# Gate and up projections of a SwiGLU FFN as 2x2 block products by Strassen's scheme, with the residual kept in DRAM meanwhile

## Chip, cores, metric

One Trainium2 chip, one of its cores. The metric is the time of one execution on the device, in microseconds. The median of three runs of the kernel before is 1309.06 us.

## The reference

One inference step of one layer on 512 prompt tokens and 8 sample tokens (520 columns together): dilated window attention and an RWKV-7 recurrence on the same normalised input, merged by gates, an output projection, and then the FFN that the change is about:

```python
x = x + mix
hn = rms_norm(x, lw['norm_ffn'])
ffn = (jax.nn.silu(hn @ lw['w_gate']) * (hn @ lw['w_up'])) @ lw['w_down']
return x + ffn
```

All is float32. `w_gate` and `w_up` are 1024 x 2816, `w_down` is 2816 x 1024; the last step is another RMS norm.

## The kernel before

Activations lie with features on the 128 partitions and the NT = 520 tokens on the free axis; a product is made in two chunks of CH = 260 columns (`CS[0]`, `CS[1]`). KD = 8 is the number of 128-row blocks of 1024, KF = 22 that of 2816.

Every float32 factor is split into a high part rounded to `fp32r` and a low part, and a product is the sum of three passes: high by high, high by low, low by high (`gemm_chunk`). One output tile of 128 features over 1024 inputs is thus 2 chunks x 8 blocks x 3 passes = 48 matmuls, each with its own weight load of 128 x 128 and 260 moving columns.

The work of TensorE is a list of `Job`s that `play` goes through: while it multiplies job i, it fetches the raw weights of job i+2 (`wraw`: one DMA of 512 KB on SP's queue, two buffers) and splits those of job i+1 (`wsplit`: ScalarE copies raw to `whi`, VectorE subtracts to `wlo`; two pairs of buffers). Behind a job comes its `post`, which takes the result from PSUM. Side chains (norms, for one) are generators that `Weave` mixes into the list by planned times; `wv.set` and `wv.until` are its flags. Instructions of one engine run in the order written down for it at build time, and semaphores between engines do the rest.

The end of the kernel in order:

- `w_out`, 8 jobs. `wo_pre` loads the input into `x2` (8 DMAs on POOL's queue), `wo_post` adds the product to `x2`, writes a scaled split of it into the last 8 blocks of the FFN's buffers `fh`/`fl` (`ff["h"]`, `ff["l"]`), and adds up the squares.
- `norm2`, a side chain: the reciprocal root `rs`, then for each of 8 blocks `x2 * g * rs` (VectorE, tile `hf`) and its split into `h2h`/`h2l`, the low part in turn on VectorE and on GpSimd (POOL).
- gate and up, 22 tiles each, alternately. The first EARLY = 3 pairs don't wait for `norm2`: they multiply the split from `wo_post`, and `rs` is multiplied in afterwards. The other 19 pairs multiply `h2h`/`h2l`. `gt_post` makes silu from tanh (ScalarE) and one VectorE operation for each chunk; `up_post` multiplies by the up result and splits the product into `fh`/`fl`.
- `w_down`, 8 output tiles over 22 blocks; `down_post` adds to `x2`, and `final` normalises and stores.

All operations go through one helper, so that the profile gives line 380 for every one of them; the tiles' names tell them apart. In the profile `sl` is the silu tile, `mm`, `ax` and `ch` are PSUM banks.

Of the kernel before, what the change touches and what calls it, by code (L numbers as in the profile page):

```python
# [8 lines left out]
FP = mybir.dt.float32  # L9
# [30 lines left out]
MERGE_AT = -1  # L40
SAMPLE_AT = -1
PLAIN = 4
EARLY = 3
FETCH = 2
SOLVERS = 2
RAWS = 4
# [419 lines left out]
def program(tc, I, O):  # L466
# [29 lines left out]
    def bank():  # L496
        return axp.tile([128, 512], FP, name=nm("ax"), tag="ax", bufs=3)
# [48 lines left out]
            E.matmul(ps[:cols, :n], lhsT=hi[:, k, :cols], rhs=b, start=False, stop=False)  # L546
            E.matmul(ps[:cols, :n], lhsT=lo[:, k, :cols], rhs=a, start=False, stop=(last and k == nk - 1))

    def play(jobs, more=None):
        raws, ws = {0: first_raw, 1: second_raw}, {0: first_w}  # L550

        def fetch(i, j):
            while len(jobs) <= max(i, j) and more:
# [1161 lines left out]
                                   op0=ALU.mult, op1=ALU.subtract)  # L1715
        return post

    mctx, fctx = ExitStack(), ExitStack()
# [27 lines left out]
    def wo_post(n):  # L1746
        def post(ps):
            x2 = ff["x2"]
            for c in range(2):
                V.tensor_tensor(out=x2[:, n, CS[c]], in0=x2[:, n, CS[c]], in1=ps[c][:, :CH], op=ALU.add)  # L1750

            g = feat[:, F_FFN, n:n + 1]
            S.activation(out=ff["h"][:, K0 + n], in_=x2[:, n], func=AF.Copy, scale=g)
            V.scalar_tensor_tensor(out=ff["l"][:, K0 + n], in0=x2[:, n], scalar=g, in1=ff["h"][:, K0 + n].bitcast(FP),
                                   op0=ALU.mult, op1=ALU.subtract)
            sumsq(ff["acc"], x2[:, n], n)
            if n == KD - 1:
                wv.spawn(norm2())
        return post

    def norm2():
        mctx.close()
        hp2 = ff["hp2"] = pool("h2", h2ctx, side="right")
        hh2 = ff["hh"] = hp2.tile([128, KD, NT], FR, name="h2h")
        hl2 = ff["hl"] = hp2.tile([128, KD, NT], FR, name="h2l")
        banks = yield from norm_r(ff["xp"], [ff["acc"]], slice(0, NT), TB, "f")
        for a, b, pb in banks:
            S.copy(out=ff["rs"][:, a:b], in_=pb[:, :b - a])
        wv.set("rs2")
# [13 lines left out]

    def gt_post(n):
        def post(ps):
            xp = ff["xp"]
            t = ff["t", n] = xp.tile([128, NT], FP, name=nm("sl"), tag="sl", bufs=2)
            for c in range(2):
                g = ps[c][:, :CH]
                if n < EARLY:  # L1790
                    gs = xp.tile([128, CH], FP, name=nm("g0"), tag="g0")
                    V.tensor_tensor(out=gs[:], in0=g, in1=ff["rs"][:, CS[c]], op=ALU.mult)
                    g = gs[:]
                S.activation(out=t[:, CS[c]], in_=g, func=AF.Tanh, scale=0.5)
                V.scalar_tensor_tensor(out=t[:, CS[c]], in0=t[:, CS[c]], scalar=1.0, in1=g, op0=ALU.add, op1=ALU.mult)
        return post

    def up_post(n):
        def post(ps):
            t = ff["t", n]  # L1800
            for c in range(2):
                V.tensor_tensor(out=t[:, CS[c]], in0=t[:, CS[c]], in1=ps[c][:, :CH], op=ALU.mult)
            if n < EARLY:
                V.tensor_tensor(out=t[:], in0=t[:], in1=ff["rs"][:], op=ALU.mult)
            S.activation(out=ff["h"][:, n], in_=t[:], func=AF.Copy, scale=0.5)
            V.scalar_tensor_tensor(out=ff["l"][:, n], in0=t[:], scalar=0.5, in1=ff["h"][:, n].bitcast(FP),
                                   op0=ALU.mult, op1=ALU.subtract)
# [160 lines left out]
```

## Time and profile before

| what | value |
|---|---|
| median of 3 runs | 1309.06 us (1307.44 to 1310.26) |
| the profiled execution | 1316.53 us, of which the span from first to last instruction is 1314.8 us |
| granted TensorE clock, mean of the span | 0.983 |
| matmuls in the span | 11738 |
| matmuls that read `h2h` or `h2l` | 1824 (3 x 608), first start 954.4 us, last start 1171.9 us |

PE is TensorE's matmuls, PEld its weight loads, DVE VectorE, ACT ScalarE, POOL GpSimd, SP the engine whose queue loads the weights. In rows of the timeline the first number is the start in us, the second the duration in us, and what stands in brackets is the idle time before and what ended it. In rows of groups, the number behind x is the count, then come busy us and mean ns, and behind the last bar the engine's idle time before them. Records of VectorE overlap by some 0.08 us where one operation follows another without a wait, so its throughput is read from the distance between starts.

### The profile page before, as it was taken

What the parts mean: (1) busy time and instruction counts of PE and PEld (TensorE: products, weight loads), DVE (VectorE), ACT (ScalarE), POOL (GpSimd) and SP (SyncE); (2) the same over time, 40 slices, a digit from 0 to 9 for tenths busy, and PEclk for the clock granted to TensorE, in tenths of its full rate; (3) what the DMA queues carried; (4) which work ended last, traced back from release to release, by engine and by line L of the source; (5) the groups of instructions that cost most, each with busy time, mean ns of one, the idle gap of its engine ahead of it and who ended that gap; (6) DMA issues with size and microseconds to landing.
All of it is one profiled execution on the core that took longest, in us unless ns stands there. A gap on an engine that the chain in (4) does not pass through costs nothing.

```text
span 1314.8 us, 29468 instructions
## 1 busy us (share of the span) xinstructions
PE 1264.7 (96%) x11738; PEld 1197.5 (91%) x11738; DVE 843.7 (64%) x2221; ACT 610.6 (46%) x1554; POOL 175.0 (13%) x261
## 2 busy tenths in 40 slices
PE   7999999999989989999999999999999999999996
PEld 7998999989978878888888888999999999999996
DVE  6956866954869998886986665555843444332333
ACT  5244244366656656675785665334433232222220
POOL 1300100100223332121123122110200000000000
PEclk9999999999989999997999999999999999999998
DMA  6523654634245554543245454552222222223331
GB/s 215 158 94 96 213 178 146 221 112 172 69 131 136 152 147 141 143 156 97 77 139 168 123 175 157 182 192 85 81 97 97 97 89 89 97 93 89 89 101 65
DMA packets 92137, 169.48 MB, mean 129 GB/s; under 512 B 42416, under 2 KB 47568, under 8 KB 92000
## 3 DMA queue, kind: packets, MB, share of 16 engines
q1 hardware_dynamic: 60880, 102.46, 24.6%
q0 software_dynamic: 14512, 46.47, 11.5%
q10 hardware_dynamic: 16608, 18.68, 4.3%
q8 instruction: 92, 1.51, 0.5%
q14 instruction: 45, 0.37, 0.1%
HBM read 133.20 MB, written 27.94 MB: 123 GB/s over the span
## 4 chain that ended last, share of the span: by engine, by line
PE 64%; DVE 15%; issue 9%; DMA 6%; ACT 4%; POOL 1%; SPq 1%; ACTq 0%; DVEq 0%; POOLq 0%
PE mm L380 51%; PE ax L380 8%; PE ch L380 5%; DVE wlo L380 2%; DVE X L380 1%; DVE xt L380 1%; DMA fb<-FD 1%; DMA sw<-raw 1%; ACT KB L380 1%; DVE k L380 1%; DMA raw<-w_in 1%; SPq L380 1%; DVE raw L380 1%; DVE qk L380 1%; DVE GH L380 1%
## 5 line engine op out<-in xcount | busy, mean ns | idle before, releaser
L380 PE MATMUL mm<-hh,whi 128*128 128x260 f32 x1136 | 340.2, 299 | 0.8 <-ACT gt L380 0.8
L380 PE MATMUL mm<-hh,wlo 128*128 128x260 f32 x1136 | 325.4, 286 | 4.3 <-DVE wlo L380 4.3
L380 PE MATMUL mm<-hl,whi 128*128 128x260 f32 x1136 | 325.7, 287 | 0.0
L380 ACT CAST whi<-raw 128x1024 fp32r<-128x1024 f32 (+1 forms) x165 | 170.1, 1032 | 324.4 <-PE mm L380 290.6
L380 DVE TENSOR_TENSOR wlo<-raw,whi 128x1024 fp32r<-128x1024 f32 (+1 forms) x165 | 197.9, 1199 | 140.2 <-ACT whi L380 137.0
L380 PEld LDWEIGHTS mm<-hh,whi 128*128 128x128 f32 x1136 | 215.7, 190 | 13.3 <-issue 6.0
L380 PEld LDWEIGHTS mm<-hh,wlo 128*128 128x128 f32 x1136 | 215.4, 190 | 6.5 <-DVE wlo L380 5.8
L380 PEld LDWEIGHTS mm<-hl,whi 128*128 128x128 f32 x1136 | 215.5, 190 | 1.4 <-issue 0.2
L380 PE MATMUL mm<-h2l,whi 128*128 128x260 f32 x608 | 171.5, 282 | 0.0
L380 PE MATMUL mm<-h2h,wlo 128*128 128x260 f32 x608 | 171.4, 282 | 0.0
L380 PE MATMUL mm<-h2h,whi 128*128 128x260 f32 x608 | 171.4, 282 | 0.0
L380 PEld LDWEIGHTS mm<-h2h,wlo 128*128 128x128 f32 x608 | 114.5, 188 | 0.0
L380 PEld LDWEIGHTS mm<-h2l,whi 128*128 128x128 f32 x608 | 114.4, 188 | 0.0
L380 PEld LDWEIGHTS mm<-h2h,whi 128*128 128x128 f32 x608 | 114.4, 188 | 0.0
L380 PE MATMUL mm<-fh,wlo 128*128 128x260 f32 x388 | 109.6, 282 | 0.0
L380 PE MATMUL mm<-fh,whi 128*128 128x260 f32 x388 | 109.5, 282 | 0.0
L380 PE MATMUL mm<-fl,whi 128*128 128x260 f32 x388 | 109.5, 282 | 0.0
L380 PEld LDWEIGHTS mm<-fh,whi 128*128 128x128 f32 x388 | 73.1, 188 | 0.0
L380 PEld LDWEIGHTS mm<-fl,whi 128*128 128x128 f32 x388 | 73.0, 188 | 0.0
L380 PEld LDWEIGHTS mm<-fh,wlo 128*128 128x128 f32 x388 | 72.9, 188 | 0.0
L380 DVE TENSOR_TENSOR xt<-X,LT 128x60 f32<-128x60 f32 (+24 forms) x248 | 60.3, 243 | 3.6
L380 DVE TENSOR_TENSOR X<-X,xt 128x60 f32<-128x60 f32 (+24 forms) x248 | 57.6, 232 | 3.8
(390 smaller groups left out, 2588.8 us busy)
## 6 DMA issues: line engine op xcount, KB each, us to landing
raw<-w_in SPq DMA_DIRECT2D x77, 512.0 KB, 3.7
raw<-w_gate SPq DMA_DIRECT2D x22, 512.0 KB, 3.2
raw<-w_up SPq DMA_DIRECT2D x22, 512.0 KB, 3.2
raw<-w_down SPq DMA_DIRECT2D x16, 512.0 KB, 3.5
kt<-kcache POOLq DMA_DIRECT2D x24, 256.0 KB, 3.7
kt<-vcache POOLq DMA_DIRECT2D x24, 256.0 KB, 3.5
sw<-raw ACTq DMA_DIRECT2D x64, 65.0 KB, 3.6
GD<-gt ACTq DMA_DIRECT2D x16, 260.0 KB, 3.0
```

Source lines behind the costliest of these rows:

```text
L380: r = f(*a, **k)
```

## The change

From the fifth pair on (EARLY becomes 4), gate tile n and up tile n are multiplied together. Each of the two weight tiles is cut into its upper and lower 512 inputs, and the normalised input into the two chunks of 260 columns, which gives a 2x2 block product; Strassen's scheme (in Winograd's form) makes it from seven block products of 4 input blocks each, in place of eight.

- The factors' sums: `norm2` now makes seven blocks of 260 columns for each of 4 pairs of input blocks (four subtractions on POOL, tile `z`, then splits); `pairs` makes four weight sums `S1` to `S4` for each pair (128 x 512 each, on POOL) and splits seven weight blocks of 128 x 512 (cast on ScalarE, subtraction on VectorE, for the fifth block on POOL).
- The products' sums: seven additions on VectorE, each with one operand in PSUM, into `p1`, `q6` and `u3`.
- Memory: `x2` is written to DRAM (`X2D`) block by block in `wo_post`, its space is given to raw weights, sums and results, and it is loaded again (`x2b`) when `w_down` begins. Four blocks of `fh`/`fl` take the space of `z`.

The diff, cut to this:

```diff
-EARLY = 3
+EARLY = 4
...
-    def play(jobs, more=None):
-        raws, ws = {0: first_raw, 1: second_raw}, {0: first_w}
+    def play(jobs, raws, ws, more=None):
...
+    X2D = drp.tile([128, KD, NT], FP, name="X2D")
...
     def wo_pre():
         rctx.close()
         gctx.close()
         xp = pool("x2", ctx)
-        ff["x2"] = x2 = xp.tile([128, KD, NT], FP, name="x2")
-        for k in range(KD):
-            G.dma_start(out=x2[:, k], in_=I["xT"][:, k])
         ff["acc"] = xp.tile([128, NT], FP, name="accf")
         ff["rs"] = xp.tile([128, NT], FP, name="rsf")
         ff["xp"] = xp
         fp = pool("ff", fctx)
-        ff["h"] = fp.tile([128, KF, NT], FR, name="fh")
-        ff["l"] = fp.tile([128, KF, NT], FR, name="fl")
+        for x in "hl":
+            a, b = (fp.tile([128, n, NT], FR, name=nm("f" + x)) for n in (EARLY, KF - EARLY - 4))
+            ff[x] = [a[:, k] for k in range(EARLY)] + [None] * 4 + [b[:, k] for k in range(KF - EARLY - 4)]
+        ff["fp"] = fp
+        ff["x2"] = x2 = pool("x2", xctx).tile([128, KD, NT], FP, name="x2")
+        for k in range(KD):
+            G.dma_start(out=x2[:, k], in_=I["xT"][:, k])
         yield ()
...
-            S.activation(out=ff["h"][:, K0 + n], in_=x2[:, n], func=AF.Copy, scale=g)
-            V.scalar_tensor_tensor(out=ff["l"][:, K0 + n], in0=x2[:, n], scalar=g, in1=ff["h"][:, K0 + n].bitcast(FP),
+            S.activation(out=ff["h"][K0 + n], in_=x2[:, n], func=AF.Copy, scale=g)
+            V.scalar_tensor_tensor(out=ff["l"][K0 + n], in0=x2[:, n], scalar=g, in1=ff["h"][K0 + n].bitcast(FP),
                                    op0=ALU.mult, op1=ALU.subtract)
             sumsq(ff["acc"], x2[:, n], n)
+            G.dma_start(out=X2D[:, n], in_=x2[:, n])
             if n == KD - 1:
                 wv.spawn(norm2())
...
-        hh2 = ff["hh"] = hp2.tile([128, KD, NT], FR, name="h2h")
-        hl2 = ff["hl"] = hp2.tile([128, KD, NT], FR, name="h2l")
+        hh2 = ff["hh"] = hp2.tile([128, KD // 2, 7, CH], FR, name="h2h")
+        hl2 = ff["hl"] = hp2.tile([128, KD // 2, 7, CH], FR, name="h2l")
         banks = yield from norm_r(ff["xp"], [ff["acc"]], slice(0, NT), TB, "f")
         for a, b, pb in banks:
             S.copy(out=ff["rs"][:, a:b], in_=pb[:, :b - a])
         wv.set("rs2")
-        for k in range(KD):
-            t = ff["xp"].tile([128, NT], FP, name=nm("hf"), tag="sq", bufs=2)
-            V.scalar_tensor_tensor(out=t[:], in0=ff["x2"][:, k], scalar=feat[:, F_FFN, k:k + 1], in1=ff["rs"][:],
-                                   op0=ALU.mult, op1=ALU.mult)
-            split(hh2[:, k], hl2[:, k], t[:], (V, G)[k % 2])
-            wv.set("h2", k)
-            yield (hl2[:, k],)
+        for j in range(KD // 2):
+            z = ff["fp"].tile([128, 8, CH], FP, name=nm("z"), tag=f"z{j % 2}")
+            for i in range(2):
+                k = j + i * KD // 2
+                V.scalar_tensor_tensor(out=z[:, 2 * i:2 * i + 2], in0=ff["x2"][:, k].rearrange("p (b c) -> p b c", b=2),
+                                       scalar=feat[:, F_FFN, k:k + 1], in1=ff["rs"][:].rearrange("p (b c) -> p b c", b=2),
+                                       op0=ALU.mult, op1=ALU.mult)
+            for o, x, y in ((4, 1, 0), (6, 3, 1), (5, 3, 4), (7, 2, 5)):
+                G.tensor_tensor(out=z[:, o], in0=z[:, x], in1=z[:, y], op=ALU.subtract)
+            split(hh2[:, j, 0], hl2[:, j, 0], z[:, 0])
+            split(hh2[:, j, 1:3], hl2[:, j, 1:3], z[:, 2:4])
+            yield (z[:, 7],)
+            split(hh2[:, j, 3:], hl2[:, j, 3:], z[:, 4:])
+            wv.set("h2", j)
+            yield (hl2[:, j],)
+        for i, x in enumerate("hl"):
+            w = ff["fp"].tile([128, 8, CH], FR, name=nm("fz"), tag=f"z{i}")
+            ff[x][EARLY:EARLY + 4] = [w[:, 2 * k:2 * k + 2].rearrange("p a b -> p (a b)") for k in range(4)]
+        xctx.close()
+        ff["wp"] = pool("ws", sctx)
+        wv.set("ws")
...
+    def half_out(n, t):
+        S.activation(out=ff["h"][n], in_=t[:], func=AF.Copy, scale=0.5)
+        V.scalar_tensor_tensor(out=ff["l"][n], in0=t[:], scalar=0.5, in1=ff["h"][n].bitcast(FP),
+                               op0=ALU.mult, op1=ALU.subtract)
...
+    def pairs():
+        ns, K2 = range(EARLY, KF), KD // 2
+        last = 7 * len(ns)
+        raws, sums, parts = {}, {}, {}
+        yield from wv.until("ws")
+        sp_ = ff["wp"]
+        wab = [wpair(), wpair()]
+        def load(i):
+            if i < len(ns):
+                own = i % 2 == 0
+                raws[i] = [(sp_ if own else wp).tile([128, KD, 128], FP, name=nm("raw"), tag=("rg", "ru")[x] if own else "raw",
+                                                     bufs=1 if own else 2) for x in range(2)]
+                SY.dma_start(out=raws[i][0][:], in_=I["w_gate"][ns[i]])
+                SY.dma_start(out=raws[i][1][:], in_=I["w_up"][ns[i]])
+        def add(i, *which):
+            if i < len(ns):
+                g, u = raws[i]
+                s = sums.setdefault(i, {})
+                for w in which:
+                    s[w] = sp_.tile([128, K2, 128], FP, name=nm("S"), tag=f"S{w}")
+                    x, y = {1: (u[:, :K2], u[:, K2:]), 2: (s.get(1), g[:, :K2]), 3: (g[:, :K2], u[:, :K2]),
+                            4: (g[:, K2:], s.get(2))}[w]
+                    G.tensor_tensor(out=s[w][:], in0=x[:], in1=y[:], op=ALU.add if w == 1 else ALU.subtract)
+        def prep(q):
+            i, j = divmod(q, 7)
+            if q < last:
+                g, u = raws[i]
+                src = [lambda: g[:, :K2], lambda: sums[i][2][:], lambda: g[:, K2:], lambda: sums[i][3][:],
+                       lambda: u[:, K2:], lambda: sums[i][1][:], lambda: sums[i][4][:]][j]()
+                o = (q if q < last - 4 else q + (2 - last) % 4 + 0) % 4
+                hi, lo = (t[:, o % 2 * K2:o % 2 * K2 + K2] for t in wab[o // 2])
+                S.copy(out=hi, in_=src)
+                (G if j == 4 else V).tensor_tensor(out=lo, in0=src, in1=hi.bitcast(FP), op=ALU.subtract)
+                parts[q] = hi, lo
+                if j == 5:
+                    add(i + 1, 1, 2, 3)
+                elif j == 6:
+                    add(i + 1, 4)
+                    load(i + 2)
+                    if i == len(ns) - 1:
+                        down_raw.update({x: wraw(down[x]) for x in range(2)})
+        load(0)
+        load(1)
+        add(0, 1, 2, 3, 4)
+        for q in range(3):
+            prep(q)
+        xp = ff["xp"]
+        for i, n in enumerate(ns):
+            t = xp.tile([128, NT], FP, name=nm("sl"), tag="sl", bufs=2)
+            p1, q6, u3 = (sp_.tile([128, CH], FP, name=nm(w), tag=w) for w in ("p1", "q6", "u3"))
+            for j, b in enumerate((0, 4, 1, 5, 6, 3, 2)):
+                q = 7 * i + j
+                prep(q + 3)
+                ps = bank() if q % 2 else mmp.tile([128, 512], FP, name=nm("mm"), tag="mm", bufs=3)
+                yield (ps,)
+                hi, lo = parts.pop(q)
+                yield hi, lo
+                o = ps[:, :CH]
+                for k in range(K2):
+                    if i == 0:
+                        yield from wv.until("h2", k)
+                    xh, xl = ff["hh"][:, k, b], ff["hl"][:, k, b]
+                    E.matmul(o, lhsT=hi[:, k], rhs=xh, start=(k == 0), stop=False)
+                    E.matmul(o, lhsT=hi[:, k], rhs=xl, start=False, stop=False)
+                    E.matmul(o, lhsT=lo[:, k], rhs=xh, start=False, stop=(k == K2 - 1))
+                    if k == 1:
+                        yield ()
+                def plus(out, x):
+                    V.tensor_tensor(out=out, in0=x, in1=o, op=ALU.add)
+                if j == 0:
+                    S.copy(out=p1[:], in_=o)
+                elif j == 1:
+                    plus(q6[:], p1[:])
+                elif j == 2:
+                    plus(p1[:], p1[:])
+                    silu2(t[:, CS[0]], p1[:])
+                elif j == 3:
+                    plus(u3[:], q6[:])
+                elif j == 4:
+                    plus(p1[:], u3[:])
+                    V.tensor_tensor(out=t[:, CS[0]], in0=t[:, CS[0]], in1=p1[:], op=ALU.mult)
+                elif j == 5:
+                    plus(q6[:], q6[:])
+                    plus(u3[:], u3[:])
+                else:
+                    plus(q6[:], q6[:])
+                    silu2(t[:, CS[1]], q6[:])
+                    V.tensor_tensor(out=t[:, CS[1]], in0=t[:, CS[1]], in1=u3[:], op=ALU.mult)
+                    half_out(n, t)
+                yield ()
+        w = wpair()
+        wsplit(w, down_raw[0], 0, down[0].nw)
+        down_w[0] = w
...
-    for n in range(KF):
+    for n in range(EARLY):
         rest.append(Job(I["w_gate"][n], KD, up_x(n), gt_post(n), hold=(lambda: wv.until("rs2")) if n == 0 else None,
-                        bank=cbank if n == 0 else None, need={k: ("h2", k) for k in range(KD)} if n == EARLY else {}))
+                        bank=cbank if n == 0 else None))
...
     def down_pre():
+        sctx.close()
         h2ctx.close()
+        ff["x2"] = pool("x2b", ctx, side="right").tile([128, KD, NT], FP, name="x2b")
+        for k in range(KD):
+            G.dma_start(out=ff["x2"][:, k], in_=X2D[:, k])
         yield ()
...
+    def everything():
+        yield from play(jobs, {0: first_raw, 1: second_raw}, {0: first_w}, more)
+        yield from pairs()
+        yield from play(down, down_raw, down_w)
+    wv.run(everything())
```

More of the change, by code (lines that the diff above doesn't have):

```diff
@@ L1716, in pb_post @@
         return post
-    mctx, fctx = ExitStack(), ExitStack()
+    mctx, fctx, xctx, sctx = (ExitStack() for _ in range(4))
+    X2D = drp.tile([128, KD, NT], FP, name="X2D")
     ff = {}
@@ L1769, in norm2 @@
         wv.set("rs2")
-        for k in range(KD):
-            t = ff["xp"].tile([128, NT], FP, name=nm("hf"), tag="sq", bufs=2)
-            V.scalar_tensor_tensor(out=t[:], in0=ff["x2"][:, k], scalar=feat[:, F_FFN, k:k + 1], in1=ff["rs"][:],
-                                   op0=ALU.mult, op1=ALU.mult)
-            split(hh2[:, k], hl2[:, k], t[:], (V, G)[k % 2])
-            wv.set("h2", k)
-            yield (hl2[:, k],)
+        for j in range(KD // 2):
[19 more added lines that the diff above has]
+        wv.set("ws")
     h2ctx = ExitStack()
     def up_x(n):
-        return lambda: ([ff["h"][:, K0 + k] for k in range(KD)], [ff["l"][:, K0 + k] for k in range(KD)]) \
-            if n < EARLY else (ff["hh"], ff["hl"])
+        return lambda: (ff["h"][K0:], ff["l"][K0:])
     def gt_post(n):
@@ L1788, in post, with silu2 @@
             for c in range(2):
[L1789 to L1795, printed above, removed]
-        return post
+                gs = xp.tile([128, CH], FP, name=nm("g0"), tag="g0")
+                V.tensor_tensor(out=gs[:], in0=ps[c][:, :CH], in1=ff["rs"][:, CS[c]], op=ALU.mult)
+                silu2(t[:, CS[c]], gs[:])
+        return post
+    def silu2(t, g):
+        S.activation(out=t, in_=g, func=AF.Tanh, scale=0.5)
+        V.scalar_tensor_tensor(out=t, in0=t, scalar=1.0, in1=g, op0=ALU.add, op1=ALU.mult)
+    def half_out(n, t):
+        S.activation(out=ff["h"][n], in_=t[:], func=AF.Copy, scale=0.5)
+        V.scalar_tensor_tensor(out=ff["l"][n], in0=t[:], scalar=0.5, in1=ff["h"][n].bitcast(FP),
+                               op0=ALU.mult, op1=ALU.subtract)
     def up_post(n):
@@ L1802, in post @@
                 V.tensor_tensor(out=t[:, CS[c]], in0=t[:, CS[c]], in1=ps[c][:, :CH], op=ALU.mult)
[L1803 to L1807, printed above, removed]
-        return post
+            V.tensor_tensor(out=t[:], in0=t[:], in1=ff["rs"][:], op=ALU.mult)
@@ L1922, in down_x @@
         return ff["h"], ff["l"]
+    down, down_raw, down_w = [], {}, {}
     def down_pre():
+        sctx.close()
         h2ctx.close()
+        ff["x2"] = pool("x2b", ctx, side="right").tile([128, KD, NT], FP, name="x2b")
+        for k in range(KD):
+            G.dma_start(out=ff["x2"][:, k], in_=X2D[:, k])
         yield ()
@@ L1938, in program @@
             nk = min(8, KF - k0)
-            rest.append(Job(I["w_down"][n][:, k0:k0 + nk], nk, down_x, down_post(n) if k0 + nk == KF else None, k0=k0,
+            down.append(Job(I["w_down"][n][:, k0:k0 + nk], nk, down_x, down_post(n) if k0 + nk == KF else None, k0=k0,
                             first=(k0 == 0), last=(k0 + nk == KF), pre=down_pre if n == 0 and k0 == 0 else None))
@@ L1944, in program @@
             nk = min(8, KF - k0)
-            rest.append(Job(I["w_down"][KD - 1][:, k0:k0 + nk] if c == 0 else None, nk, down_x,
+            down.append(Job(I["w_down"][KD - 1][:, k0:k0 + nk] if c == 0 else None, nk, down_x,
                             down_post(KD - 1, (c,)) if k0 + nk == KF else None, k0=k0, first=(k0 == 0),
@@ L1949, in program @@
     wv.spawn(norm0(), acc0, BANK)
-    wv.run(play(jobs, more))
+    def everything():
[3 more added lines that the diff above has]
+    wv.run(everything())
     fctx.close()
```

1 line of the change is left out of this document (added).

## The prediction

> **What bounds the kernel now.** I read the head of the page first, then the chain of waits in order of time, then the FFN's stretch by windows and by tiles.
>
> ```profile
> span 1314.8 us, 29468 instructions
> ...
> 837.37 79.90 PE mm L380 x666
> ...
> 925.74 365.02 PE mm L380 x3054
> ```
>
> The chain that ended last runs from 837 us to 1291 us almost wholly over TensorE's own matmuls. In this stretch nothing but their number counts.
>
> ```profile
> 926.00:954.00 28.00, 28.00 (x235) 28.00 (x235) 26.18 (x38) 12.34 (x21) 6.81 (x4) 1.00 0.24 82
> ...
> 965.00:1165.00 200.00, 200.00 (x1679) 200.00 (x1678) 82.14 (x123) 58.26 (x88) 0.00 (x0) 1.00 0.27 92
> ...
> L380 PE MATMUL mm<-h2h,whi x608: 278/282/288, 954.4 to 1171.6; 128*128 128x260 f32 x152
> ...
> L380 PE MATMUL mm<-h2h,wlo x608: 279/282/285, 954.6 to 1171.9; 128*128 128x260 f32 x152
> ```
>
> In the windows the columns are length, PE, weight loads, DVE, ACT, POOL, granted clock, DMA share, GB/s. From 965 to 1165 us PE is busy throughout, at clock 1.00, while DVE is busy 82.14 of 200 us and POOL not at all. The second thing to see is the window 926 to 954, where `norm2` runs beside the early tiles: DVE 26.18 of 28 us, and PE still has no gap. The two tile rows give the pitch: 3 x 608 = 1824 matmuls start within 1171.9 - 954.4 = 217.5 us, 119.3 ns each; a pair of gate and up tiles (96 matmuls) costs 11.45 us.
>
> **The change, part by part.**
>
> *Matmuls.* 18 pairs go from 96 to 7 x 4 x 3 = 84, so from 11.45 to 10.02 us. 18 x 12 = 216 matmuls x 119.3 ns = 25.8 us fewer: the most that there is to win.
>
> *DVE in a pair.* Its prices, from the distance between starts:
>
> ```profile
> 925.83 1.23 DVE L380 TENSOR_TENSOR wlo<-raw,whi 128x1024 fp32r<-128x1024 f32 x1 [1.66 <-PE ch L380]
> 926.97 0.75 DVE L380 SCALAR_TENSOR_TENSOR hf<-x,feat,rsf 128x520 f32<-128x520 f32 x1
> 927.65 0.42 DVE L380 TENSOR_TENSOR g<-ch,rsf 128x260 f32<-128x260 f32 x1
> 927.98 0.75 DVE L380 SCALAR_TENSOR_TENSOR hf<-x,feat,rsf 128x520 f32<-128x520 f32 x1
> 928.65 0.70 DVE L380 TENSOR_TENSOR h2l<-hf,h2h 128x520 fp32r<-128x520 f32 x1
> 929.26 0.42 DVE L380 SCALAR_TENSOR_TENSOR sl<-sl,g 128x260 f32<-128x260 f32 x1
> 929.60 1.81 DVE L380 SCALAR_TENSOR_TENSOR hf<-x,feat,rsf 128x520 f32<-128x520 f32 x1
> ...
> 929.48 1.37 POOL L380 TENSOR_TENSOR h2l<-hf,h2h 128x520 fp32r<-128x520 f32 x1 [50.45 <-ACT h2h L380]
> ...
> 945.32 0.41 DVE L380 TENSOR_TENSOR sl<-sl,mm 128x260 f32<-128x260 f32 x1
> 945.77 1.63 DVE L380 TENSOR_TENSOR sl<-sl,rsf 128x520 f32<-128x520 f32 x1
> ```
>
> 1024 wide costs 1.14 us (925.83 to 926.97), 520 wide 0.61 (928.65 to 929.26), 260 wide 0.34 (929.26 to 929.60), so 512 wide 0.60 between the first two; an operation that needs the one before it starts 0.45 later, 0.11 more (945.32 to 945.77). A pair after the change has on DVE six weight splits of 512 (3.60), seven additions with one operand in PSUM (2.38), two silu operations and two multiplications of 260 (1.36), one split of 520 (0.61) and about two dependent steps (0.22): 8.17 us. Against 10.02 us of matmuls this would be hidden.
>
> *POOL in a pair, and what it does to DVE.* Five operations of 512: `S1` to `S4` and the fifth split. In the rows above DVE's second `hf` costs 0.75 us, the third 1.81: it starts while POOL's `h2l` runs (929.48 to 930.85) and ends 0.56 behind it. One POOL operation thus cost DVE 1.06 us. For plain float32 outputs:
>
> ```profile
> 424.50 1.04 POOL L380 TENSOR_TENSOR GH<-GH,DN 64x512 f32<-64x512 f32 x1 [6.34 <-DVE GH L380]
> ...
> 394.08 0.75 DVE L380 SCALAR_TENSOR_TENSOR k<-pb,mu,k 128x511 f32<-128x511 f32 x1
> 424.53 1.55 DVE L380 SCALAR_TENSOR_TENSOR k<-pb,mu,k 128x511 f32<-128x511 f32 x1
> ...
> 416.48 1.68 POOL L380 TENSOR_TENSOR st<-st,sg 128x512 f32<-128x512 f32 x1 [5.26 <-PE ax L380]
> ...
> 346.07 0.17 DVE L380 COPY sg<-k 128x8 f32<-128x8 f32 x1
> 417.15 1.04 DVE L380 COPY sg<-k 128x8 f32<-128x8 f32 x1
> ...
> 608.54 1.04 POOL L380 TENSOR_TENSOR GH<-GH,DN 64x512 f32<-64x512 f32 x1 [2.18 <-PE ax L380]
> ...
> 608.87 0.42 DVE L380 TENSOR_TENSOR tmp<-v,ax 128x260 f32<-128x260 f32 x1 [0.34 <-PE ax L380]
> 609.21 0.44 DVE L380 TENSOR_TENSOR xt<-X,LT 128x60 f32<-128x60 f32 x1
> ```
>
> DVE loses 1.55 - 0.75 = 0.80 to a `GH` and 1.04 - 0.17 = 0.87 to an `st`; I take 0.85 for each sum and 1.05 for the fifth split. The last three rows show the exception: `tmp`, with an operand in PSUM (`ax`), runs inside a POOL operation at its normal 0.42, and only what follows is held. So POOL's operations are free where DVE is on one of its PSUM additions, or idle. Unhidden they are 4 x 0.85 + 1.05 = 4.45 us a pair; DVE then needs 8.17 + 4.45 = 12.62. Followed in the order in which the pair is written, each POOL operation comes up beside PSUM additions: `S1` beside the `p1` addition (0.30 covered), `S2` beside `u3` (0.34), `S3` beside the next `p1` with its dependent step (0.45), `S4` beside two in a row (0.68), the fifth split beside `q6` (0.34). That leaves 2.34, and DVE at 10.51. But a POOL operation also gets in ahead of an operation with both operands in SBUF, as at 929.48. I take 2.8, nearer to the low end because of that order: DVE needs 10.97 us a pair. That is over the matmuls' 10.02, so DVE sets the pace and PE waits for weight splits, with no long gap: three products are prepared ahead. 18 x (10.97 - 11.45) = -8.6 us; with the ends, 18 x (10.51 - 11.45) = -16.9 and 18 x (12.62 - 11.45) = +21.1.
>
> By the Trainium skill, "SBUF — State Buffer", section "SBUF: two separate sides", a VectorE operation with two SBUF inputs and a GpSimd operation that reads SBUF exclude each other for the whole instruction. By whole recorded durations the sum would be 8.17 + 5.47 = 13.64 us a pair; the trace agrees in kind, but charges 0.80 to 0.87 of 1.04 us.
>
> *ACT, POOL, loads.*
>
> ```profile
> L380 ACT CAST h2h<-hf x8: 627/628/630, 927.8 to 944.8; 128x520 fp32r<-128x520 f32 x8
> L380 DVE TENSOR_TENSOR h2l<-hf,h2h x4: 685/693/704, 928.7 to 944.7; 128x520 fp32r<-128x520 f32 x4
> L380 POOL TENSOR_TENSOR h2l<-hf,h2h x4: 1314/1632/2235, 929.5 to 945.5; 128x520 fp32r<-128x520 f32 x4
> ...
> raw<-w_gate SPq DMA_DIRECT2D x22, 512.0 KB, 3.2
> ...
> x<-xT POOLq DMA_DIRECT2D x8, 260.0 KB, 4.5
> ```
>
> ACT has seven casts of 0.63 or less, one copy, two tanh and one split, about 6.3 us a pair: hidden. POOL has 4 x 1.04 + 1.31 = 5.5 us, and at its worst row (2.235) 11.2; `S2` is needed some six products (8.6 us) after its turn, so this is covered unless POOL loses every time. The raw weights come in one pair (10 us) ahead against 3.2 us landing, on SP's queue in the same number: nothing. The eight stores of `x2` on POOL's queue lie beside `w_out`, the eight loads behind the last pair beside the first down tile, 132 matmuls or 15.7 us against 4.5 us landing: taken as nothing, at most 4.5 if the first down result had to wait.
>
> *`norm2` and the start of the pairs.* Its DVE work grows from 8 x 0.68 + 4 x 0.61 = 7.9 us to 8 x 0.68 + 4 x (0.34 + 0.61 + 1.16) = 13.9. POOL gets 16 subtractions of 260 in place of 4 splits:
>
> ```profile
> 482.15 0.18 DVE L380 TENSOR_TENSOR xt<-X,LT 128x24 f32<-128x24 f32 x1
> ...
> 517.30 0.61 POOL L380 TENSOR_TENSOR svd<-uk,sel 48x256 f32<-48x256 f32 x1 [2.27 <-ACT uk L380]
> ...
> 517.33 0.61 DVE L380 TENSOR_TENSOR xt<-X,LT 128x24 f32<-128x24 f32 x1
> ```
>
> An `xt` of this width costs 0.18 (482.15), so such an operation holds DVE 0.43: 16 x 0.43 = 6.9 us against the 4 x 1.06 = 4.2 of the splits before, 2.7 more. The fourth early tile adds 5.5 us of DVE work and 11.45 us of room; the first pair's preparation adds 5.2. Demand: 26.2 + 6.0 + 2.7 + 5.5 + 5.2 = 45.6 us, room 28 + 11.45 = 39.4. Up to 6 us late, none if PSUM operations cover POOL; I take 2.
>
> ```profile
> L380 ACT CAST whi<-raw 128x1024 fp32r<-128x1024 f32 x46 | 48.3, 1050 | 142.1 <-PE mm L380 123.3 <-issue 18.8
> ```
>
> *The end of the pairs.* The first down weights need a buffer that the last products use, then a cast (1.05) and a split (1.23 at 925.83): 0 if it comes free two products early, 2.3 if at the last; I take 1.
>
> **The sum.** -8.6 + 2 + 1 = -5.6 us. The profiled execution took 1316.53 us, 7.5 above the median of the runs, and would come to 1310.9; against the median of 1309.06 it is **1303 us** (1303.5).
>
> **The rivals.**
>
> *The matmuls set the pace (0.14).* If POOL's operations fall wholly beside PSUM additions and idle time, a pair costs 10.02: -25.8 + 3 = -23, 1286 us. For it: DVE alone is at 8.17. Against it: the room for 4.45 us of POOL is 2.38 us of additions and 1.85 of idle time, all of which would have to fit.
>
> *POOL's sums are paid in full (0.31).* 12.62 us a pair, +21.1 + 3 = +24, 1333 us, slower. It decides from a loss of 3.1 us a pair on: 18 x (8.17 + 3.1 - 11.45) + 3 = 0. For it: in the FFN the POOL operation at 945.53 came up beside a PSUM operation and still cost `sl` 1.63 - 0.70 = 0.93 (0.70 for 520 wide at 928.65):
>
> ```profile
> 945.53 1.31 POOL L380 TENSOR_TENSOR h2l<-hf,h2h 128x520 fp32r<-128x520 f32 x1 [2.31 <-ACT h2h L380]
> ```
>
> Against it: the order described above.
>
> *The whole instruction excludes (0.04).* 13.64 us a pair, +39.4 + 3, 1351 us. The rows at 424.53 and 417.15 speak against it. It is the rule of "SBUF — State Buffer" taken by its word.
>
> *A late start of the pairs (0.09).* `norm2` ends the full 6 us late, POOL's in-order sums for the first pair behind it cost four times 1.04 more, and the end pays 2.3: +12.5 in place of +3, 1313 us. Against it: PE had no gap at 26.18 of 28 us of DVE.
>
> **How the numbers follow.** A measurement of this kernel tells 0.2%, 2.6 us, from no change. The likeliest case, DVE and POOL alternating at 10.5 to 11.4 us a pair, has 0.42 and its own range 1294 to 1312; of it 0.33 is faster, 0.07 the same, 0.02 slower. The matmuls' pace gives 0.14 faster; the sums in full 0.03 same and 0.28 slower; the exclusion 0.04 slower; the late start 0.01, 0.03 and 0.05. Together 0.48 faster, 0.13 same, 0.39 slower. The range reaches from the matmuls' pace, 1285, to the sums in full, 1332; above and below are left some 2 in 10.
>
> **What would show it.** In the windows of the pairs DVE near full, PE at 0.90 to 0.95, POOL at more than half; weight loads that wait for the `wlo` split; DVE splits of 512 in two sizes, 0.68 and about 1.2 to 1.5 us. PE without gaps would show the first rival; a pitch over 11.45 us a pair the second; a gap ahead of the first product of `h2h` the late start. Most likely wrong is the 2.8: how often POOL's turn falls on a PSUM addition.

## The result, and the profile after

The kernel after the change took 1346.76 us (median of 4 runs, 1342.27 to 1347.59), the kernel before 1309.66 us beside it (4 runs, 1307.44 to 1312.10): ratio 1.0276, 95% interval 1.0246 to 1.0305. It is slower, and 44 us from the forecast of 1303, past the upper end of the range too. The profiled execution took 1346.47 us, about its median; that of before lay 7 us above the median of its runs, so the spans below differ by 29.9 us where the medians differ by 37.

PE's busy tenths in 40 slices on the page of the kernel before, then the page of the kernel after: span, busy time, and the busy tenths of 40 slices of 33.6 us.

```profile
PE   7999999999989989999999999999999999999996
```

```profile
span 1344.7 us, 29616 instructions
...
PE 1252.9 (93%) x11522; PEld 1175.2 (87%) x11522; DVE 990.0 (74%) x2430; ACT 653.0 (49%) x1666; POOL 323.3 (24%) x379
...
PE   7999999999989989989999999999988888889996
...
DVE  6947967944689988878886655657899999982234
POOL 1200101100242231211221221202465555540000
```

216 matmuls are gone (11738 to 11522). In the slices 29 to 35, counted from 0, PE stands at 8 where it stood at 9 before, DVE is at 9 (8 in the last), and POOL works about half of the time. The same by windows (length, PE, weight loads, DVE, ACT, POOL, granted clock, DMA share, GB/s): `norm2` with the early tiles, the stretch up to the first pair, the pairs.

```profile
926.00:954.00 28.00, 25.02 (x205) 24.39 (x203) 27.11 (x37) 13.20 (x21) 14.61 (x15) 1.00 0.24 76
954.00:972.00 18.00, 15.96 (x120) 15.96 (x121) 14.78 (x20) 5.95 (x10) 9.50 (x6) 0.91 0.35 118
972.00:1201.40 229.40, 195.42 (x1514) 185.25 (x1514) 215.73 (x320) 98.42 (x196) 123.06 (x86) 1.00 0.25 79
```

The first and the last product of the pairs, in the tile rows of the kernel after:

```profile
L380 PE MATMUL mm<-h2h,whi x252: 277/282/289, 972.1 to 1199.6; 128*128 128x260 f32 x126
...
L380 PE MATMUL ax<-h2h,wlo x252: 278/283/394, 973.7 to 1201.3; 128*128 128x260 f32 x126
```

From 972.1 to 1201.3 us are 229.2 us for 18 pairs: 12.73 us each, against 11.45 before. The forecast was 10.97. One pair on DVE (start, duration; in brackets the idle time before and what ended it), cut to the rows that show something:

```profile
1093.03 0.99 DVE L380 SCALAR_TENSOR_TENSOR fl<-sl,fh 128x520 fp32r<-128x520 f32 x1 [0.70 <-ACT fh L380]
...
1094.28 0.68 DVE L380 TENSOR_TENSOR wlo<-S,whi 128x512 fp32r<-128x512 f32 x1
...
1095.22 1.66 DVE L380 TENSOR_TENSOR wlo<-S,whi 128x512 fp32r<-128x512 f32 x1
1096.81 1.50 DVE L380 SCALAR_TENSOR_TENSOR sl<-sl,p 128x260 f32<-128x260 f32 x1
1098.23 0.41 DVE L380 TENSOR_TENSOR u<-q,mm 128x260 f32<-128x260 f32 x1
1098.57 1.43 DVE L380 TENSOR_TENSOR wlo<-raw,whi 128x512 fp32r<-128x512 f32 x1
...
1103.52 0.42 DVE L380 SCALAR_TENSOR_TENSOR sl<-sl,q 128x260 f32<-128x260 f32 x1
1103.98 1.40 DVE L380 TENSOR_TENSOR sl<-sl,u 128x260 f32<-128x260 f32 x1
1106.09 0.99 DVE L380 SCALAR_TENSOR_TENSOR fl<-sl,fh 128x520 fp32r<-128x520 f32 x1 [0.70 <-ACT fh L380]
```

And POOL in the same pair:

```profile
1095.04 1.29 POOL L380 TENSOR_TENSOR S<-raw 128x512 f32<-128x512 f32 x1 [1.57 <-DVE wlo L380]
1096.41 1.61 POOL L380 TENSOR_TENSOR S<-S,raw 128x512 f32<-128x512 f32 x1
1098.10 1.34 POOL L380 TENSOR_TENSOR S<-raw,S 128x512 f32<-128x512 f32 x1
...
1103.68 1.41 POOL L380 TENSOR_TENSOR S<-raw,raw 128x512 f32<-128x512 f32 x1 [4.24 <-DVE wlo L380]
1105.05 1.46 POOL L380 TENSOR_TENSOR wlo<-raw,whi 128x512 fp32r<-128x512 f32 x1
```

By their operands the sums are `S1` (`raw`), `S2` (`S,raw`), `S4` (`raw,S`) and `S3` (`raw,raw`). So POOL's order is not that of the source: the build has put `S3` ahead of the fifth split. A split of 512 takes 0.68 where POOL is idle (1094.28). `S1` starts at 1095.04, and the split at 1095.22 takes 1.66; `S2` at 1096.41, and `sl` at 1096.81 takes 1.50 in place of 0.42; `S4` at 1098.10: the PSUM addition at 1098.23 inside it takes its normal 0.41, and the split behind that 1.43; `S3` at 1103.68 catches the multiplication of `sl` by `u` (1.40 in place of 0.42), the fifth split `fl` (0.99 in place of 0.69). The losses are 0.98 + 1.08 + 0.74 + 0.98 + 0.30 = 4.08 us. With the forecast's own work of 8.17 and the 0.70 us in which DVE waits for ScalarE's `fh`, that makes 12.95 of the 13.06 us from one `fl` to the next. For a sum that came late DVE waited nowhere in this pair.

The ends of the rows show how the two take turns. Each of the five held DVE rows ends behind the POOL row that holds it by nearly its own length: 0.29 us where it is 260 wide, 0.55 to 0.57 where it is 512 or 520 wide. And `S2`, `S4`, `S3` and the fifth split end 1.13 to 1.15 us behind the DVE row of two SBUF operands that ran before them, whatever their recorded length (1.34 to 1.61): part of that length is POOL's own wait for DVE.

That this holds for all pairs is seen in DVE's groups of the pairs' stretch (count | busy us, mean ns | idle before), and in the list of waits (total us, times, longest). TensorE's 34.0 us without matmuls in this stretch are 25.9 us of waits for DVE's splits and 8.1 for POOL's fifth split:

```profile
L380 DVE TENSOR_TENSOR wlo<-S,whi 128x512 fp32r<-128x512 f32 x71 | 65.5, 922 | 0.1
L380 DVE TENSOR_TENSOR wlo<-raw,whi 128x512 fp32r<-128x512 f32 x35 | 36.6, 1046 | 0.0
L380 DVE SCALAR_TENSOR_TENSOR sl<-sl,p 128x260 f32<-128x260 f32 x18 | 26.0, 1446 | 0.0
L380 DVE TENSOR_TENSOR sl<-sl,u 128x260 f32<-128x260 f32 x17 | 22.9, 1346 | 0.6
L380 DVE SCALAR_TENSOR_TENSOR fl<-sl,fh 128x520 fp32r<-128x520 f32 x14 | 13.7, 976 | 9.2 <-ACT fh L380 9.2
```

```profile
PE ax L380 <- DVE wlo L380: 13.0, 16, 1.4
PE mm L380 <- DVE wlo L380: 12.9, 16, 1.4
...
PE ax L380 <- POOL wlo L380: 4.1, 8, 0.5
PE mm L380 <- POOL wlo L380: 4.0, 8, 0.5
```

The start of the pairs: the first step of `norm2`'s reciprocal root in the kernel before, then in the kernel after, and two of the gaps of PE behind it.

```profile
922.00 0.17 DVE L380 TENSOR_SCALAR nv<-ax 104x5 f32<-104x5 f32 x1 [1.18 <-PE ax L380]
```

```profile
920.87 0.17 DVE L380 TENSOR_SCALAR nv<-ax 104x5 f32<-104x5 f32 x1 [1.17 <-PE ax L380]
...
939.55 0.39 PE L380 MATMUL mm<-fh,wlo 128*128 128x260 f32 x1 [1.97 <-DVE wlo L380]
...
956.04 0.39 PE L380 MATMUL mm<-fh,whi 128*128 128x260 f32 x1 [2.09 <-DVE g L380]
```

Before, the first pair that waits for `norm2` began 954.4 - 922.0 = 32.4 us behind `nv`; a fourth early pair makes that 43.85. It is 972.1 - 920.87 = 51.2: 7.4 us late. So the spans' 29.9 us are: up to `nv` -1.1, late start +7.4, pairs 229.2 - 18 x 11.45 = +23.1, and the end +0.5 (143.4 us from the last product on, against 142.9).

### The profile page after: what moved, and what is told of

The parts are those of the page before. It is cut to its first block, busy times and chain, and to the rows that moved or that the text cites. A ratio compares the mean times of both kernels' runs of the same rounds, so it can differ in the third digit from the quotient of the medians.

```text
span 1344.7 us, 29616 instructions
## 1 busy us (share of the span) xinstructions
PE 1252.9 (93%) x11522; PEld 1175.2 (87%) x11522; DVE 990.0 (74%) x2430; ACT 653.0 (49%) x1666; POOL 323.3 (24%) x379
## 4 chain that ended last, share of the span: by engine, by line
PE 42%; DVE 25%; issue 16%; DMA 6%; POOL 6%; ACT 5%; SPq 1%; ACTq 0%; DVEq 0%; POOLq 0%
PE mm L380 30%; PE ax L380 7%; DVE wlo L380 5%; PE ch L380 5%; DVE sl L380 3%; POOL S L380 3%; DMA fb<-FD 1%; DVE X L380 1%; DVE xt L380 1%; DMA sw<-raw 1%; DMA kt<-vcache 1%; POOL wlo L380 1%; DVE qk L380 1%; DVE k L380 1%; DVE raw L380 1%
## 5 line engine op out<-in xcount | busy, mean ns | idle before, releaser
L380 PE MATMUL mm<-fh,whi 128*128 128x260 f32 x364 | 103.7, 285 | 3.0 <-DVE g L380 2.1
L380 PE MATMUL mm<-fl,whi 128*128 128x260 f32 x364 | 103.5, 284 | 0.0
L380 PE MATMUL ax<-h2h,wlo 128*128 128x260 f32 x252 | 74.4, 295 | 17.1 <-DVE wlo L380 13.0
L380 PE MATMUL mm<-h2h,wlo 128*128 128x260 f32 x252 | 74.4, 295 | 16.9 <-DVE wlo L380 12.9
L380 PE MATMUL ax<-h2l,whi 128*128 128x260 f32 x252 | 71.2, 282 | 0.0
L380 PE MATMUL mm<-h2h,whi 128*128 128x260 f32 x252 | 71.1, 282 | 0.0
L380 PE MATMUL mm<-h2l,whi 128*128 128x260 f32 x252 | 71.1, 282 | 0.0
L380 PE MATMUL ax<-h2h,whi 128*128 128x260 f32 x252 | 71.1, 282 | 0.0
L380 PEld LDWEIGHTS ax<-h2h,wlo 128*128 128x128 f32 x252 | 47.3, 188 | 22.1 <-DVE wlo L380 16.4
L380 PEld LDWEIGHTS mm<-h2h,wlo 128*128 128x128 f32 x252 | 47.3, 188 | 22.0 <-DVE wlo L380 16.2
```

Source lines behind the costliest of these rows:

```text
L380: r = f(*a, **k)
```

## The experiments

Three theories of the pairs' pace were to be told apart: POOL's operations hold DVE; the products wait for sums that POOL finishes late; DVE's own work is too long. Diffs are against the kernel after the change, where nothing else is said. The kernel before had medians of 1309.95, 1310.90 and 1312.15 us (19, 7 and 11 runs) beside the three groups in which the runs were made. The diffs are shortened, some lines are put together, and comments are added.

**No work on POOL in the pairs.** The kernel leaves out the sums; raw blocks stand in their place, and the numbers that it computes are others.

```diff
-            if i < len(ns):                      # add()
+            if i < 0:
...
-                src = [... sums[i][2][:] ... ][j]()
+                src = [g[:, :K2], g[:, :K2], g[:, K2:], u[:, :K2], u[:, K2:], u[:, :K2], g[:, K2:]][j]
...
-                (G if j == 4 else V).tensor_tensor(out=lo, ...)
+                V.tensor_tensor(out=lo, ...)
```

> The pairs without any work on POOL: the weight sums S1 to S4 are left out (the blocks of raw weights stand in their place, which changes the numbers computed), and the fifth split runs on VectorE. Theory 1, POOL's operations hold VectorE's: VectorE has 8.17 + 0.60 = 8.8 us a pair and some 0.7 of waiting left, under the 10.0 us of matmuls, so a pair falls from 12.75 to about 10.1 us and the time from 1346.8 to about 1299 us, below the kernel before. Theory 2, POOL's sums come late and the splits wait for them: the same 1299. Theory 3, VectorE's own operations are too many whatever POOL does: the pair stays above 12 us, over 1330 us.

Measured: 1292.34 us (1291.58 to 1293.10), ratio to before 0.9851 (0.9801 to 0.9902). Its window in the pairs and its first and last product:

```profile
990.00:1150.00 160.00, 159.49 (x1328) 159.16 (x1327) 147.38 (x299) 92.98 (x171) 1.88 (x4) 1.00 0.31 100
```

```profile
L380 PE MATMUL mm<-h2h,whi x252: 277/282/288, 966.3 to 1146.0; 128*128 128x260 f32 x126
...
L380 PE MATMUL ax<-h2h,wlo x252: 278/283/294, 968.0 to 1147.7; 128*128 128x260 f32 x126
```

PE has no gaps, and a pair takes 181.4 / 18 = 10.08 us. DVE does all seven splits and still has room. Its own work is not what slows the pairs; what POOL does, in one way or the other, costs 54 us. Of the 24.7 us that the pairs gain on the kernel before, 17.6 reach the time: here too the pairs begin some 7 us late (51.1 us behind `nv`), since `norm2`'s subtractions are still on POOL.

**The sums made, but read by nobody.** As above in `src` alone.

> POOL makes S1 to S4 and the fifth split as in the changed kernel, but nobody reads the sums: the casts and splits take raw blocks in their place (which changes the numbers computed). Theory 1, POOL's operations hold VectorE's: POOL's work is the same, so a pair stays at 12.2 to 12.8 us, 1337 to 1347 us. Theory 2, the splits wait for late sums: nothing waits any more, a pair falls to about 10.2 us, 1300 us.

Measured: 1355.04 us (1350.70 to 1359.38), ratio 1.0329 (1.0264 to 1.0394), 8 us above the range that theory 1 gave. That nobody waits for the sums brought nothing, which speaks against late sums as the cause. But the run isn't clean: POOL's in-order sums now waited for the raw loads (100.8 us from 964 to 1220 us), the fifth split behind them held TensorE (35.0 us), and the granted clock of 990 to 1140 us was 0.91. So a cleaner form followed:

**Subtractions on POOL that nobody reads.** The kernel without POOL's work, and five subtractions in each pair, of two raw blocks into a spare tile. POOL makes them as soon as a pair's raw weights have landed: these loads are what it waits for.

```diff
                 parts[q] = hi, lo
+                if j in (1, 2, 3, 5, 6):
+                    d = sp_.tile([128, K2, 128], FP, name=nm("dm"), tag="dm")
+                    G.tensor_tensor(out=d[:], in0=g[:, :K2], in1=u[:, :K2], op=ALU.subtract)
```

> The pairs without POOL (sums left out, as before), to which five POOL subtractions of 128 x 512 a pair are added that read two blocks of raw weights already in SBUF and write a tile that nobody reads. Nothing waits for them, apart from the raw buffers' release. Theory 1, POOL's reading operations hold VectorE: 8.8 + 4 to 5 us, a pair goes from 10.08 to 12.5 to 13.5 us, 1335 to 1352 us. Theory 2, late sums: nothing is late, 10.1 us a pair, 1292 us.

Measured: 1351.83 us (one run). A window in the pairs, then three groups of DVE from 1000 to 1180 us; below, two groups of the kernel without POOL's work, from 1000 to 1140 us:

```profile
990.00:1140.00 150.00, 118.16 (x922) 112.16 (x921) 149.24 (x212) 60.16 (x121) 82.35 (x55) 1.00 0.24 77
...
L380 DVE TENSOR_TENSOR wlo<-raw,whi 128x512 fp32r<-128x512 f32 x94 | 94.0, 1000 | 0.0
...
L380 DVE SCALAR_TENSOR_TENSOR fl<-sl,fh 128x520 fp32r<-128x520 f32 x11 | 19.5, 1775 | 0.0
...
L380 DVE TENSOR_TENSOR q<-q,mm 128x260 f32<-128x260 f32 x13 | 5.4, 417 | 0.0
```

```profile
L380 DVE TENSOR_TENSOR wlo<-raw,whi 128x512 fp32r<-128x512 f32 x98 | 67.6, 689 | 3.6
L380 DVE SCALAR_TENSOR_TENSOR fl<-sl,fh 128x520 fp32r<-128x520 f32 x12 | 8.4, 701 | 1.4
```

Work that nobody waits for costs 1351.8 - 1292.3 = 59 us. The splits go from 689 to 1000 ns in the mean, `fl` from 701 to 1775; the additions with an operand in PSUM stay at 417 ns (425 without POOL's work), and DVE is full. This shows that POOL holds DVE, and that this alone is enough.

**Writes on POOL alone.** The same, with a memset of 128 x 1280 in place of the subtraction.

> The pairs without POOL (sums left out), to which five POOL memsets of 128 x 1280 a pair are added: they write SBUF and read nothing, and nothing waits for them, so POOL runs them one behind the other over the first half of the pairs. Theory 1 in its narrow form, only a POOL operation that reads SBUF holds VectorE: VectorE's splits of 512 stay at 0.68 us and a pair at 10.1 us, 1292 us. Rival, any POOL work holds VectorE: while the memsets run, splits of up to 1.6 us and over 11 us a pair, 1305 us or more.

Measured: 1295.11 us (one run). A window in the pairs, then the rows of the splits and of the memsets (count: shortest/median/longest ns, first to last start):

```profile
975.00:1040.00 65.00, 65.00 (x544) 65.00 (x543) 60.37 (x123) 37.85 (x71) 61.94 (x54) 1.00 0.35 113
```

```profile
L380 DVE TENSOR_TENSOR wlo<-raw,whi x45: 684/692/694, 975.3 to 1038.7; 128x512 fp32r<-128x512 f32 x45
...
L380 POOL MEMSET dm<- x90: 1164/1169/1179, 949.6 to 1060.3; 128x1280 f32 x90
```

POOL is busy 61.94 of 65 us, more than ever with the sums, and no split is longer than 694 ns. PE has no gap in this window, and the 18 pairs take 181.4 us, 10.08 each, as without any work on POOL. How long POOL works doesn't matter; what holds DVE is work that reads SBUF, which the memsets don't. By the Trainium skill, "SBUF — State Buffer", section "Who interferes with whom", a VectorE instruction with two SBUF inputs contends with a GpSimd instruction that reads SBUF, and not with one that only writes it; the trace agrees (684 to 694 ns beside the memsets, 1000 in the mean beside the subtractions).

**The sums and the fifth split on DVE.** `G` becomes `V` in `add` and in the split.

> S1 to S4 and the fifth split on VectorE, nothing on POOL in the pairs. Theory 1: VectorE has 8.17 + 5 x 0.60 = 11.17 us a pair and 0.7 of waiting for ScalarE, 11.9 in place of 12.75: 18 x -0.85 = -15 us, about 1331 us; VectorE's splits of 512 all 0.68 us. Theory 2: the sums come no later than VectorE's turn, the pair falls to the matmuls' 10.2, 1300 us. If POOL cost VectorE nothing, moving 3 us a pair to VectorE would make it slower, over 1380 us.

Measured: 1314.39 us (10 runs, 1310.01 to 1322.68), ratio 1.0021 (0.9995 to 1.0048). A window in the pairs (its last 5 us lie behind them), and a group of DVE from 1000 to 1150 us:

```profile
990.00:1170.00 180.00, 169.27 (x1341) 162.95 (x1340) 175.34 (x363) 89.71 (x172) 4.28 (x8) 1.00 0.30 93
...
L380 DVE TENSOR_TENSOR wlo<-S,whi 128x512 fp32r<-128x512 f32 x53 | 36.2, 683 | 0.0
```

Five more operations on DVE, and 32 us less: 5 x 0.60 = 3.0 us of work replace 4.08 us of losses and the 0.70 us wait for `fh`, which other work now fills. One `fl` follows the other after 11.36 us, and 8.17 + 3.0 + 0.20 of waiting make 11.37; over all 18 pairs it is 11.12. I had expected 1331 us, with the wait counted in full. DVE sets the pace still, so this equals the kernel before and gains nothing.

**The change's side parts alone:** the kernel before with the fourth early pair, the stores of `x2` and their reload.

```diff
-EARLY = 3
+EARLY = 4
...
+    X2D = drp.tile([128, KD, NT], FP, name="X2D")
...
+            G.dma_start(out=X2D[:, n], in_=x2[:, n])
...
+        for k in range(KD):
+            G.dma_start(out=ff["x2"][:, k], in_=X2D[:, k])
```

> The kernel before with only the side parts of the change: EARLY = 4, and x2 stored to DRAM block by block behind w_out and loaded again when w_down begins. Theory 1: these cost nothing, within 2.6 us of the kernel before (1309). Rival: the store and load or the later start take part of the 37 us: 5 us or more slower.

Measured: 1313.27 us (10 runs, 1310.29 to 1319.33), ratio 1.0025 (0.9998 to 1.0051): 3.3 us, a little over the 2.6 that I had allowed, at most 0.5%, and not told from nothing.

**`norm2`'s subtractions on DVE.**

```diff
-                G.tensor_tensor(out=z[:, o], in0=z[:, x], in1=z[:, y], op=ALU.subtract)
+                V.tensor_tensor(out=z[:, o], in0=z[:, x], in1=z[:, y], op=ALU.subtract)
```

> The changed kernel with norm2's sixteen subtractions on VectorE in place of POOL, and nothing else changed: the pairs keep POOL's sums. Theory 1: TensorE's gaps ahead of the pairs (5 us between 926 and 957) go, the pairs stay at 12.7 us each, 4 to 6 us faster than the changed kernel (1346.8), 1341 to 1343 us. Rival: the late start comes from VectorE's own larger norm2, the gaps stay, 1347 us.

Measured: 1338.69 us (1334.93 to 1346.58), ratio 1.0208 (1.0167 to 1.0250), 8 us below the change. The same stretch of `norm2`, the first step of the root, and the first product of the pairs:

```profile
926.00:954.00 28.00, 27.81 (x231) 27.50 (x230) 27.54 (x53) 13.53 (x22) 0.33 (x1) 1.00 0.39 132
...
914.15 0.17 DVE L380 TENSOR_SCALAR nv<-ax 104x5 f32<-104x5 f32 x1 [1.17 <-PE ax L380]
...
L380 PE MATMUL mm<-h2h,whi x252: 277/282/289, 958.6 to 1188.8; 128*128 128x260 f32 x126
```

PE is all but without gaps although DVE has 16 operations more, and the pairs begin 958.6 - 914.2 = 44.4 us behind `nv`: 0.5 late, not 7.4. So nearly all of the late start was POOL's subtractions. The pairs themselves stay slow, 12.9 us each.

**Fewer additions.** Products in the order `(0, 2, 1, 5, 3, 6, 4)`, several added up in one PSUM bank: products 0, 1, 3, 4 in bank A, 5 and 6 in C. ScalarE copies the intermediate states that are needed again, and four of the seven additions go. Sums and splits are on DVE.

```diff
-            for j, b in enumerate((0, 4, 1, 5, 6, 3, 2)):
+            for pos, j in enumerate(ORD):            # ORD = (0, 2, 1, 5, 3, 6, 4)
...
+                if pos == 0:   A_ = ps = mmp.tile(...)
+                elif pos == 1: B_ = ps = bank()
+                elif pos == 3: C_ = ps = bank()
+                else:          ps = C_ if pos == 5 else A_
+                fresh = pos in (0, 1, 3)
...
-                    E.matmul(o, lhsT=hi[:, k], rhs=xh, start=(k == 0), stop=False)
+                    E.matmul(o, lhsT=hi[:, k], rhs=xh, start=(fresh and k == 0), stop=False, ...)
...
+                elif pos == 2: S.copy(out=q6[:], in_=o)          # A: products 0 and 1
+                elif pos == 3: S.copy(out=u3[:], in_=o)          # C: product 5
+                elif pos == 4: V.tensor_tensor(out=u3[:], in0=u3[:], in1=o, op=ALU.add)
+                elif pos == 5: V.tensor_tensor(out=q6[:], in0=q6[:], in1=o, op=ALU.add)
...
+                else: V.tensor_tensor(out=t[:, CS[0]], in0=t[:, CS[0]], in1=o, op=ALU.mult)
+                    late.append((n, t))              # half_out behind the next pair's first product
```

> All sums and splits on VectorE, and the products added up in PSUM where they can be: the products are made in the order 0, 2, 1, 5, 3, 6, 4 in three banks, so that four go onto one bank and two onto another, with ScalarE copying what is needed in between; VectorE adds three times a pair in place of seven, and the last split of a tile is written behind the next tile's first product. Theory 1, VectorE's own work sets the pace once POOL is out: 7 x 0.60 + 4 x 0.60 + 4 x 0.34 + 2 x 0.34 + 0.34 + 0.61 + 0.2 = 9.8 us a pair, under the matmuls' 10.08, so a pair costs 10.1 to 10.4 and the time is 1314.4 - 18 x 0.8 = about 1300 us. Rival: TensorE waits for ScalarE's copies of an open bank, over 11.1 us a pair, 1314 us or more.

Measured: 1292.67 us (1291.85 to 1295.55), ratio 0.9858 (0.9812 to 0.9905); 10.1 us a pair, at the matmuls' pace; 7 us below what I had expected.

**The same with the sums and the fifth split on POOL.**

> The same order and banks, but S1 to S4 and the fifth split on POOL, as in the changed kernel. Theory 1: VectorE's own work is 6 x 0.60 + 4 x 0.34 + 2 x 0.34 + 0.34 + 0.61 + 0.2 = 6.8 us a pair, and POOL's five operations cost it 4 to 5 us, since four PSUM additions that could stand beside them are gone: 10.9 to 11.8 us a pair, 1313 to 1330 us, slower than with all on VectorE although VectorE has 3 us less to do. Rival, POOL's operations fit into VectorE's idle time: 10.1 us a pair, 1300 us.

Measured: 1335.64 us (1328.72 to 1337.62), ratio 1.0179 (1.0130 to 1.0227), 6 us above what was expected; 12.2 us a pair. The window of the pairs with POOL, and a wait of its queue; below, the window of the one with all on DVE:

```profile
990.00:1140.00 150.00, 135.62 (x1018) 131.57 (x1017) 135.53 (x169) 78.28 (x157) 92.48 (x60) 0.93 0.25 87
...
POOL S L380 <- DMA raw<-w_up: 45.1, 11, 5.5
```

```profile
990.00:1140.00 150.00, 150.00 (x1252) 150.00 (x1251) 146.80 (x284) 96.38 (x194) 0.00 (x0) 1.00 0.31 99
```

The engine of five operations (and the place of the sums, one product earlier) is worth 43 us even where DVE has four additions fewer. That POOL's queue waited for loads, and that the clock was 0.93, is seen; how much each adds to the hold was not separated.

**All on DVE, `norm2` too:** the chained version with the edit of `norm2` from above.

> As the kernel with PSUM chains and all on VectorE, and norm2's sixteen subtractions of 260 on VectorE too. Theory 1: on POOL they hold VectorE some 0.5 us each, on VectorE they cost 0.34 each: TensorE's gaps between 926 and 954 us (5 us in the kernels with POOL there) shrink to 1 to 3 us, 2 to 4 us faster than without, about 1297 us. Rival: VectorE is the bound there either way, no change.

Measured: 1291.99 us (1288.20 to 1295.41), ratio 0.9855 (0.9808 to 0.9901), where I had expected about 1297. Run again:

> The kernel with PSUM chains, nothing on POOL in the FFN, measured again with more rounds: 1288 to 1296 us, 1.1 to 1.7% under the kernel before.

Measured: 1286.20 us (6 runs, 1282.31 to 1295.93) against 1312.15 (11 runs), ratio 0.9820 (0.9776 to 0.9863), 2 us below the range expected. It beats the kernel before by 1.8%, and by the two ratios the change by 4.4%. Next to the chained version with `norm2`'s subtractions on POOL (1292.67), the intervals of the whole time don't tell whether `norm2` adds something. The profiled executions do show the start: the pairs begin 44.4 us behind `nv` with these subtractions on DVE, 50.5 with them on POOL.

## Why the prediction was wrong, by its own steps

- *Matmuls, 10.02 us a pair:* right. Without POOL's work in them a pair takes 10.08, and the pairs gain the full 25 us.
- *DVE's own work, 8.17 us:* right; with measured losses and waits the period closes to 0.1 us.
- *POOL's effect on DVE, 2.8 us: this step failed.* The mechanism was right, the size was not: 4.08 us. The price without cover was not far off, 4.45 against 4.08: the four sums cost 0.74 to 1.08, 3.78 together where the forecast had 3.40, and the fifth split 0.30 where it had 1.05, since it came mostly while DVE waited for `fh`. What failed is the 1.65 us taken off for cover by PSUM additions. I followed the order of the source and found each POOL operation beside such additions. In the trace the order is another: `S3` and the fifth split come beside the two `sl` operations and `fl`, none of which reads PSUM. And an addition takes 0.41 us where a POOL operation takes 1.13 behind DVE's row, so POOL holds the operation behind the addition for the rest, as `S4` did (0.74). Priced in full, as the second rival had it, the step would have been nearly right.
- *DVE's wait for ScalarE, 0:* it was left out. DVE needs `sl`'s product, then `fh`, before `fl`: 0.70 us a pair (9.2 us in 13), since nothing was queued between. Step and losses together are 4.78 us, over the 3.1 from which the second rival decides.
- *The start, +2 (up to 6):* measured 7.4. With these subtractions on DVE it is 0.5, so their hold was mis-sized, not the rest of `norm2`'s work: the 0.43 came from a POOL row of 0.61 us (48x256), and the subtractions' own rows took 0.80 to 1.73. The early tiles' `wlo` and `g` stood behind held operations, and PE had gaps of 1.97 and 2.09 us for them. From 954 to 972 us the granted clock was 0.91, worth 18 x 0.09 = 1.6 us at most.
- *The end, +1:* 0.5. *Loads, ACT, `x2`:* nothing that can be told from no change, as taken.
- *The rivals:* the second (12.62 us a pair, 1333 us) came nearest by its pace, with 12.73 measured. With the late start as measured its sum is 21.1 + 7.4 + 1 = +29.5, against the spans' 29.9. The late start of the fourth rival came on top of it. Of the exclusion for whole instructions the price is not borne out (13.64 us a pair): POOL's 7.11 us of recorded work in the pair shown cost DVE 4.08, since part of it is POOL's own wait, and part lies beside PSUM additions and DVE's wait for `fh`. The exclusion itself is what the ends of the rows show. The prediction read its rows against it ("0.80 to 0.87 of 1.04"), but the 0.87 belongs to an `st` of 1.68 us that began 0.67 us before the copy, and `k` ended 0.54 behind the `GH`, as the 512 wide rows do here. That this rival's 1351 us lies nearest to the measured time is luck: its pairs are too slow by 0.9 us each, 16 us in all, and what makes up for it is a start 5.4 us too early in its sum and the 7 us by which the medians differ more than the spans.
- *What would show it:* splits in two sizes (0.68 and 1.43 to 1.66), weight loads that wait for `wlo`, DVE near full (0.94) and POOL over half (0.54) came as said; PE was at 0.85, not 0.90 to 0.95. The pitch of 12.73 us was over 11.45, the mark of the second rival, and the gaps ahead of the first product were that of the late start.

## What to carry to other kernels

Moving elementwise work with two SBUF operands to GpSimd did not unload VectorE here: five operations cost VectorE 4.08 us there and 3.0 us on its own queue. Count such an operation in full against VectorE unless a trace of the same kernel shows the cover, and don't take the cover from the order of the source: the build may set the operations down in another. Look first for additions that can be dropped altogether (products of one chain added up in a PSUM bank) before moving any.

## What the runs showed of the chip that was not expected

- A GpSimd addition or subtraction of 128 x 512 with two full SBUF operands took 1.29 to 1.61 us by its record in the pair shown, and among the unread subtractions 1.60 in the middle and up to 2.16. Part of it is its wait for VectorE: counted from the end of VectorE's row it was 1.13 to 1.15. VectorE's own record of such an operation is 0.68, 0.60 from start to start.
- What counts is reading: memsets that kept GpSimd busy 95% of the time left PE without a gap, subtractions that nobody reads cost 59 us in the time.
- A PSUM bank that ScalarE has copied from can go on accumulating the next product, at no loss of pace: 1252 matmuls in 150.00 us in the chained version, 119.8 ns each.
